# Moving the chunk mask of the attention into spare channels, and moving small work between engines

## The chip, the cores and the metric

The kernel runs on one core of a Trainium2 chip. The metric is device time in microseconds (us); below, TensorE is PE, VectorE is DVE (in the code `V`), ScalarE is ACT (`S_`), GpSimd is POOL (`G`), and SP issues most of the DMAs. The kernel before takes 921.42 us, the median of 3 runs (921.26 to 925.33).

## What is computed

Two layers of a hybrid trunk over 1024 tokens of width 1024, in float32. Each layer normalises its input, projects it with one combined weight, runs three branches (a gated linear recurrence, multi-head latent attention, a spatial gating unit), gates and normalises them, projects them back and adds the residual. The change touches the attention branch:

```python
q = (rms_norm(q_lat, q_norm_g) @ w_uq).reshape(B, S, 6, 96)      # 64 plain + 32 rotary channels
k = concat(k_nope[6 heads x 64], k_pe[32, the same for all heads])
q_pe, k_pe = apply_rope(...)      # (x1 cos - x2 sin, x2 cos + x1 sin), halves of 16
s = q @ k.T * 96 ** -0.5
mask = k_chunk[None, :] <= q_chunk[:, None]      # chunks of 64 tokens
p = softmax(where(mask, s, -inf));  o = p @ v
yb = o * silu(gb)
```

With blocks of 128 queries, the mask leaves out all later blocks of keys; inside the block of the diagonal it hides the second 64 keys from the first 64 queries.

## The kernel before, in words

Every float32 product is made of three matmuls on parts (`mm3`, L123 to L126): a value is split into a rounded high part (ACT writes it) and the remainder (DVE or GpSimd subtracts, `split`, L355 to L358). All matmuls have a stationary operand of 128 by 128.

Per layer, in order: the recurrence's projections, the gating unit's, the latent projection (`toks`, L764 to L800, one step per 128 tokens, which also rotates the shared keys into `ln` and transposes them), then the gate of the attention branch with the loading of `w_uq` (`load_uq`), then the attention, then the output projection (`project`).

The heads use 128 channels per query and key: 64 plain ones, and 64 that carry the rotation as four products of 16 (`cos`, `cos`, `-sin`, `sin`), prepared by a table `MQ` with which each query is multiplied after its projection (`queries`, L893), and by doubled key sums (L776).

The attention runs over 24 units (head h, pair of query blocks j). The loop `for n in range(len(units))` issues, per turn, keys and queries for unit n + 4, `scores` for unit n + 2, and `mixv` for unit n. `scores` makes for each of two blocks i: the score matmuls into one of two PSUM buffers (`pw`), a matmul of the identity with `mask_b` that adds -1e30 on the hidden corner (L929), the negated row maximum on DVE (L936), the exponential on ACT with the row sum (L938), the reciprocal on DVE (L939) and the multiplication by it on GpSimd (L940). `mixv` transposes the probabilities (L960), splits them (L357, L358), multiplies them with the values (L969) into one half of a PSUM buffer `o`, adds the two halves of the partitions (ACT L977, DVE L978) and multiplies the gate in (L981, on DVE for the 13 units of `Y_ON_V`, on GpSimd for the 11 others). `Q_ON_V` lists the queries that DVE splits.

The order of the instructions on each engine isn't that of the program text: a planner with its own costs for each instruction (`schedule_with_timeline_sim=True`) lays them out when the kernel is built, except for those under `keep`. Each engine then runs its list strictly in order.

Of the kernel before, what the change touches and what calls it, by code (L numbers as in the profile page):

```python
# [25 lines left out]
YA, YC, YB = 0, 3, 5  # L26

TWO_PI = 2.0 * np.pi
EXP_C = (1.0, 0.5, 1.0 / 6, 1.0 / 24, 1.0 / 120, 1.0 / 720, 1.0 / 5040)
# [9 lines left out]
W_ON_V = (C_U, C_GC)  # L39
Q_ON_V = ((0, 0), (0, 1), (1, 1), (4, 0))  # L40
Y_ON_V = (2, 4, 5, 6, 8, 9, 13, 14, 16, 19, 20, 21, 23)
# [46 lines left out]
def trunk_kernel(tc, A, out):  # L88
# [54 lines left out]
    G.memset(mhalf, -0.5)  # L143
    mask_b = cst.tile([128, 256], F32R, name="mask_b")
    G.memset(mask_b.bitcast(F32), 0.0)
    G.memset(mask_b[0:64, 192:256].bitcast(F32), -1e30)
    Y = cst.tile([128, 8, T], F32, name="Y")
# [107 lines left out]
    def rope_tables():  # L255
# [44 lines left out]
        V.memset(TQ[:, :, 0:64], SCALE)  # L300
        for o, tab, c in ((64, CK, SCALE), (80, CK, SCALE), (96, SK, -SCALE), (112, SK, SCALE)):
            V.tensor_scalar(out=TQ[:, :, o:o + 16], in0=tab, scalar1=c, scalar2=None, op0=ALU.mult)
        for h in range(2):
# [247 lines left out]
    for l in range(DEPTH):  # L551
# [210 lines left out]
        for t in range(NT):  # L762
            if t % 2 == 0:
                latn.append(FS.take((128, 2, 384)))  # L764
            ln = latn[t // 2][:, t % 2]
            ps = toks(hT, w, t, 352, "P1")
# [8 lines left out]
            V.tensor_tensor(out=r2[:, 1, 16:32], in0=kr[:, 0:16], in1=SK[:, t], op=ALU.mult)  # L775
            V.tensor_tensor(out=ln[:, 192:256].rearrange("p (a b) -> p a b", a=2),  # L776
                            in0=r2[:, 0:1].to_broadcast([128, 2, 32]), in1=r2[:, 1:2].to_broadcast([128, 2, 32]),
                            op=ALU.add)
            r = rsqrt(ms, 2)
# [28 lines left out]
        def load_uq(r0, n, gcol):  # L808
# [4 lines left out]
            g = par[:, gcol:gcol + 1]  # L813
            for o, i, c in ((96, 80, 16), (112, 64, 16), (0, 0, 96)):
                V.tensor_scalar(out=st[:, :, o:o + c], in0=st[:, :, i:i + c], scalar1=g, scalar2=None, op0=ALU.mult)
            i = len(uq)
# [69 lines left out]
        def queries(h, half):  # L886
# [5 lines left out]
            qm = HS.take((128, 512))  # L892
            V.tensor_tensor(out=qm, in0=ps, in1=MQ[:, hs], op=ALU.mult)  # L893
            q = RS.take((128, 2, 512))
# [9 lines left out]
        def scores(h, j):  # L904
# [5 lines left out]
            else:  # L910
                pair = None
            res = []
            for i in (2 * j, 2 * j + 1):
                n = (i + 1) * 128
                o = (i % 4) * 128
                sh, sl = q[:, 0, o:o + 128], q[:, 1, o:o + 128]
                ps = bank("P2") if j >= 2 else pw[:, (i % 2) * 512:(i % 2 + 1) * 512]

                step = n // 2 if n == 640 else 512
                for c0 in range(0, n, step):  # L920
                    w = max(256, min(step, n - c0))
                    diag = c0 <= i * 128 < c0 + step
                    o0 = c0 // step * 512
                    mm3(ps[:, o0:o0 + w], sh, sl, kh[:, c0:c0 + w], kl[:, c0:c0 + w], True, not diag)
                    if diag:

                        d1 = o0 + (i + 1) * 128 - c0
                        d0 = max(o0, d1 - 256)
                        PE.matmul(ps[:, d0:d1], lhsT=identr, rhs=mask_b[:, 256 - (d1 - d0):256], start=False,  # L929
                                  stop=True)  # L930
                if step < 512:
                    sv = ps.rearrange("p (a b) -> p a b", b=512)[:, :, 0:step]
                else:
                    sv = ps[:, 0:n].rearrange("p (a b) -> p a b", a=1)
                mx, sm, rs = SM(1), SM(1), SM(1)
                V.tensor_reduce(out=mx, in_=sv, axis=AX.XY, op=ALU.max, negate=True)  # L936
                p = FS.take((128, 1024)) if j >= 2 else pair[:, i % 2]
                S_.activation(p[:, 0:n].rearrange("p (a b) -> p a b", a=sv.shape[1]), sv, AF.Exp, bias=mx, accum_out=sm)  # L938
# [9 lines left out]
        def mixv(h, j):  # L948
# [27 lines left out]
            tmp = HS.take((128, 256))  # L976
            S_.activation(tmp[mine], o[other], AF.Copy, scale=0.5)  # L977
            V.scalar_tensor_tensor(out=tmp[mine], in0=o[mine], scalar=0.5, in1=tmp[mine],  # L978
                                   op0=ALU.mult, op1=ALU.add)
            yv = Y[mine, YB + h // 2, j * 256:(j + 1) * 256]  # L980
            (V if units.index((h, j)) in Y_ON_V else G).tensor_tensor(out=yv, in0=yv, in1=tmp[mine], op=ALU.mult)  # L981
            HS.give(tmp)
# [174 lines left out]
```

## Time and profile before

| What | us |
|---|---|
| median of 3 runs | 921.42 |
| the profiled execution, its own time | 919.1 |
| its span, first to last instruction | 917.3 |
| PE busy in it | 877.1 |
| DVE busy | 583.9 |
| ACT busy | 520.3 |
| POOL busy | 395.1 |
| granted TensorE clock, mean | 0.994 |

A busy time is the union of an engine's instructions. A matmul's row lasts longer than the slot that it takes: matmuls overlap each other in the array, so that the price of one is read from the distance of two starts, and short waits don't show as idle time. The attention takes about 255 to 380 us in layer 0 and 699 to 825 us in layer 1 (first to last mask matmul).

### The profile page before, as it was taken

The page shows a single profiled execution, that of the slowest core. Times are in us where ns is not written, and L with a number is a line of the kernel's source. Part 1 is how long each engine was busy: PE and PEld are TensorE (multiplying, and loading weights), DVE is VectorE, ACT ScalarE, POOL GpSimd, SP SyncE. Part 2 cuts the span into 40 slices and gives each one's busy share as a digit, 9 for nine tenths or more (in the row PEclk, how much of TensorE's full clock was granted, in tenths as well). Part 3 has the DMA queues.
Part 4 walks back from the last instruction along what each step waited for, and adds up shares of the span by engine and source line. Part 5 has one row for each costly group of instructions (what it writes and reads, how often), then busy time and mean ns, then how long its engine had stood idle before and what let it go on. Part 6 is the DMA issues. An engine that isn't in the chain of part 4 may idle for free. (4 is left out here: it accounts for less than half of the span.)

```text
span 917.3 us, 13660 instructions
## 1 busy us (share of the span) xinstructions
PE 877.1 (96%) x5078; PEld 777.1 (85%) x5078; DVE 583.9 (64%) x1092; ACT 520.3 (57%) x1032; POOL 395.1 (43%) x447
## 2 busy tenths in 40 slices
PE   4999998999999999999999999989989999999996
PEld 3998787998889889888798888889978999988886
DVE  4567955735689898356566498334555989855533
ACT  6446744554767778446444386354466877755312
POOL 4720047564045568356333000675530567655601
PEclk9999999999999999999999999999999999999999
DMA  7201366322000253024323033762200015221321
GB/s 276 56 25 44 108 215 201 132 93 60 14 1 1 93 184 111 9 88 161 106 81 100 1 88 95 275 224 110 59 14 0 1 47 200 77 70 70 138 92 69
DMA packets 45079, 86.93 MB, mean 95 GB/s; under 512 B 8824, under 2 KB 26836, under 8 KB 45012
## 3 DMA queue, kind: packets, MB, share of 16 engines
q1 hardware_dynamic: 35796, 52.50, 18.3%
q0 software_dynamic: 6912, 25.17, 7.8%
q10 hardware_dynamic: 2304, 8.39, 2.3%
q8 instruction: 40, 0.66, 0.3%
q14 instruction: 27, 0.22, 0.1%
HBM read 60.88 MB, written 25.17 MB: 94 GB/s over the span
## 5 line engine op out<-in xcount | busy, mean ns | idle before, releaser
L124 PE MATMUL pw<-R,R 128*128 128x512 f32 (+1 forms) x704 | 258.9, 368 | 6.8 <-DVE R L358 2.4
L126 PE MATMUL pw<-R,R 128*128 128x512 f32 (+1 forms) x704 | 252.7, 359 | 0.1
L125 PE MATMUL pw<-R,R 128*128 128x512 f32 (+1 forms) x704 | 252.7, 359 | 0.0
L124 PE MATMUL pa<-R,R 128*128 128x512 f32 (+3 forms) x540 | 187.2, 349 | 7.9 <-DVE F L708 3.7
L125 PE MATMUL pa<-R,R 128*128 128x512 f32 (+3 forms) x540 | 186.0, 345 | 0.0
L126 PE MATMUL pa<-R,R 128*128 128x512 f32 (+3 forms) x540 | 185.1, 345 | 0.0
L124 PEld LDWEIGHTS pw<-R,R 128*128 128x128 f32 x704 | 134.6, 192 | 26.7 <-ACT F L938 2.7
L126 PEld LDWEIGHTS pw<-R,R 128*128 128x128 f32 x704 | 134.4, 191 | 18.5 <-POOL R L377 0.5
L125 PEld LDWEIGHTS pw<-R,R 128*128 128x128 f32 x704 | 134.8, 192 | 17.2
L124 PEld LDWEIGHTS pa<-R,R 128*128 128x128 f32 x540 | 102.0, 189 | 18.6 <-DVE F L708 3.9
L940 POOL TENSOR_SCALAR F<-F,ring 128x128 f32<-128x128 f32 (+3 forms) x96 | 72.6, 761 | 89.5 <-DVE ring L939 88.1
L126 PEld LDWEIGHTS pa<-R,R 128*128 128x128 f32 x540 | 101.8, 189 | 9.9
L125 PEld LDWEIGHTS pa<-R,R 128*128 128x128 f32 x540 | 102.2, 189 | 8.4
L358 DVE TENSOR_TENSOR R<-pa,R 128x512 fp32r<-128x512 f32 (+1 forms) x120 | 73.9, 629 | 16.5 <-ACT R L357 15.6
L938 ACT ACTIVATE F<-pw,ring 128x128 f32<-128x128 f32 (+3 forms) x96 | 71.1, 743 | 21.0 <-DVE ring L936 18.4
L936 DVE TENSOR_REDUCE ring<-pw 128x1 f32<-128x128 f32 (+3 forms) x96 | 71.6, 749 | 11.4 <-PE pw L929 10.8
L377 POOL TENSOR_TENSOR R<-F,R 128x1024 fp32r<-128x1024 f32 (+1 forms) x24 | 55.2, 2307 | 45.8 <-ACT R L376 45.8
L357 ACT ACTIVATE R<-pa 128x512 fp32r<-128x512 f32 (+1 forms) x120 | 63.7, 554 | 19.6 <-PE pa L960 17.8
L969 PE MATMUL pa<-R,R 128*128 128x256 f32 x480 | 72.1, 288 | 0.5 <-DVE R L358 0.5
L969 PEld LDWEIGHTS pa<-R,R 128*128 128x128 f32 x480 | 63.5, 190 | 3.6 <-DVE R L358 1.1
L960 PE MATMUL pa<-ident,F 128*128 128x128 f32 x432 | 63.6, 273 | 0.7 <-DVE H L893 0.4
L318 ACT ACTIVATE H<-F 128x1024 bf16<-128x1024 f32 (+2 forms) x33 | 31.4, 953 | 55.6 <-DVE F L1004 33.4
(302 smaller groups left out, 1360.5 us busy)
## 6 DMA issues: line engine op xcount, KB each, us to landing
F<-in_w_in SPq DMA_DIRECT2D x24, 512.0 KB, 4.4
F<-in_x SPq DMA_DIRECT2D x13, 512.0 KB, 5.4
F<-in_w_out SPq DMA_DIRECT2D x9, 512.0 KB, 3.5
F<-x SPq DMA_DIRECT2D x8, 512.0 KB
Y<-in_w_out SPq DMA_DIRECT2D x7, 512.0 KB, 3.6
x<-F SPq DMA_DIRECT2D x7, 512.0 KB, 4.1
out_y<-F SPq DMA_DIRECT2D x7, 512.0 KB, 2.7
Y<-in_w_in SPq DMA_DIRECT2D x6, 512.0 KB, 3.6
```

The source lines that it names most:

```text
L124: PE.matmul(ps, lhsT=sh, rhs=mh, start=start, stop=False)
L125: PE.matmul(ps, lhsT=sh, rhs=ml, start=False, stop=False)
L126: PE.matmul(ps, lhsT=sl, rhs=mh, start=False, stop=stop)
L318: order(S_.activation(q.bitcast(BF16)[:, c], xs[i % len(xs)].rearrange("p a b -> p (a b)")[:, c], AF.Square, scale=1.0 / 32, accum_out=ms[ ...
L357: S_.activation(h, src, AF.Copy)
L358: (eng or G).tensor_tensor(out=lo, in0=src, in1=h.bitcast(F32), op=ALU.subtract)
L377: self.eng.tensor_tensor(out=lo, in0=st, in1=h.bitcast(F32), op=ALU.subtract)
L936: V.tensor_reduce(out=mx, in_=sv, axis=AX.XY, op=ALU.max, negate=True)
L938: S_.activation(p[:, 0:n].rearrange("p (a b) -> p a b", a=sv.shape[1]), sv, AF.Exp, bias=mx, accum_out=sm)
L940: G.tensor_scalar(out=p[:, 0:n], in0=p[:, 0:n], scalar1=rs, scalar2=1.0, op0=ALU.mult, op1=ALU.mult)
L960: PE.transpose(pv[:, c, i * 128:(i + 1) * 128], p[i][:, b * 128:(b + 1) * 128], ident)
L969: PE.matmul(o, lhsT=sv, rhs=pt[:, part, c * 256:(c + 1) * 256], start=(b == 0 and part == 0), stop=(b == nb - 1 and part == 1))
```

## The change

The hidden corner is written as a product: the query gets one extra channel per block of 128 tokens (channels 112 to 119), which is 1 for the first 64 queries of its block and 0 elsewhere; the key gets -2^100 in the same channel for the second 64 keys of its block. To free 16 channels, the rotation is written with three products of 16 in place of four. The mask matmul and `mask_b` go. The ones reach the queries through the table `MQ` and a constant column `qoff` that is added in the multiplication by `MQ`.

Beside this: the two blocks of a unit share one reciprocal (2 columns) after both exponentials; for the 13 units of `Y_ON_V` the sum of the two halves of `o` is made by a second ACT copy and a GpSimd addition, where DVE did it in one instruction; and of the four queries per layer that DVE split, two go to GpSimd.

```diff
-Q_ON_V = ((0, 0), (0, 1), (1, 1), (4, 0))
+Q_ON_V = ((0, 0), (0, 1))
...
-    G.memset(mask_b.bitcast(F32), 0.0)
-    G.memset(mask_b[0:64, 192:256].bitcast(F32), -1e30)
+    mkey = cst.tile([128, NT, 16], F32, name="mkey")
+    G.memset(mkey, 0.0)
+    G.memset(mkey.rearrange("p t f -> p (t f)")[64:128, 0::17], HIDE)
+    qoff = cst.tile([128, 1], F32, name="qoff")
+    V.tensor_reduce(out=qoff, in_=ident[:, QMASK:QMASK + 8], axis=AX.X, op=ALU.add)
...
-        for o, tab, c in ((64, CK, SCALE), (80, CK, SCALE), (96, SK, -SCALE), (112, SK, SCALE)):
-            V.tensor_scalar(out=TQ[:, :, o:o + 16], in0=tab, scalar1=c, scalar2=None, op0=ALU.mult)
+        V.tensor_scalar(out=TQ[:, :, 96:112], in0=SK, scalar1=SCALE, scalar2=None, op0=ALU.mult)
+        for o, op in ((64, ALU.subtract), (80, ALU.add)):
+            V.scalar_tensor_tensor(out=TQ[:, :, o:o + 16], in0=CK, scalar=SCALE, in1=TQ[:, :, 96:112], op0=ALU.mult,
+                                   op1=op)
+        V.memset(TQ[:, :, QMASK:128], 0.0)
+        V.memset(TQ.rearrange("p t f -> p (t f)")[0:64, QMASK::129], 1.0)
...
+                G.tensor_copy(latn[-1][:, :, 240:256], mkey[:, t:t + 2])
...
-            V.tensor_tensor(out=ln[:, 192:256].rearrange("p (a b) -> p a b", a=2),
-                            in0=r2[:, 0:1].to_broadcast([128, 2, 32]), in1=r2[:, 1:2].to_broadcast([128, 2, 32]),
-                            op=ALU.add)
+            V.tensor_tensor(out=ln[:, 192:224], in0=r2[:, 0], in1=r2[:, 1], op=ALU.add)
+            V.tensor_tensor(out=ln[:, 224:240], in0=ln[:, 192:208], in1=ln[:, 208:224], op=ALU.add)
...
-            for o, i, c in ((96, 80, 16), (112, 64, 16), (0, 0, 96)):
-                V.tensor_scalar(out=st[:, :, o:o + c], in0=st[:, :, i:i + c], scalar1=g, scalar2=None, op0=ALU.mult)
+            V.tensor_scalar(out=st[:, :, 0:96], in0=st[:, :, 0:96], scalar1=g, scalar2=None, op0=ALU.mult)
+            V.tensor_tensor(out=st[:, :, 96:112], in0=st[:, :, 64:80], in1=st[:, :, 80:96], op=ALU.subtract)
+            V.memset(st[:, :, QMASK:128], 0.0)
...
-            V.tensor_tensor(out=qm, in0=ps, in1=MQ[:, hs], op=ALU.mult)
+            V.scalar_tensor_tensor(out=qm, in0=ps, scalar=qoff, in1=MQ[:, hs], op0=ALU.add, op1=ALU.mult)
...
-                    mm3(ps[:, o0:o0 + w], sh, sl, kh[:, c0:c0 + w], kl[:, c0:c0 + w], True, not diag)
-                    if diag:
-                        d1 = o0 + (i + 1) * 128 - c0
-                        d0 = max(o0, d1 - 256)
-                        PE.matmul(ps[:, d0:d1], lhsT=identr, rhs=mask_b[:, 256 - (d1 - d0):256], start=False,
-                                  stop=True)
+                    mm3(ps[:, o0:o0 + w], sh, sl, kh[:, c0:c0 + w], kl[:, c0:c0 + w], True, True)
...
-                V.reciprocal(out=rs, in_=sm)
-                G.tensor_scalar(out=p[:, 0:n], in0=p[:, 0:n], scalar1=rs, scalar2=1.0, op0=ALU.mult, op1=ALU.mult)
                 res.append(p)
+            V.reciprocal(out=rs, in_=sm)
+            for i, p in enumerate(res):
+                n = (2 * j + i + 1) * 128
+                G.tensor_scalar(out=p[:, 0:n], in0=p[:, 0:n], scalar1=rs[:, i:i + 1], scalar2=1.0, op0=ALU.mult,
+                                op1=ALU.mult)
...
+            on_v = units.index((h, j)) in Y_ON_V
+            S_.activation(tmp[mine, 0], o[other], AF.Copy, scale=0.5)
+            if on_v:
+                S_.activation(tmp[mine, 1], o[mine], AF.Copy, scale=0.5)
+                G.tensor_tensor(out=tmp[mine, 0], in0=tmp[mine, 1], in1=tmp[mine, 0], op=ALU.add)
+            else:
+                V.scalar_tensor_tensor(out=tmp[mine, 0], in0=o[mine], scalar=0.5, in1=tmp[mine, 0],
+                                       op0=ALU.mult, op1=ALU.add)
+            (V if on_v else G).tensor_tensor(out=yv, in0=yv, in1=tmp[mine, 0], op=ALU.mult)
```

## Rows read from the trace of the kernel before

**Rows 1.** The page's first part: busy time, share of the span and instructions of each engine.

```profile
PE 877.1 (96%) x5078; PEld 777.1 (85%) x5078; DVE 583.9 (64%) x1092; ACT 520.3 (57%) x1032; POOL 395.1 (43%) x447
```

**Rows 2.** Windows: busy time (and instructions) of each engine in the dense stretch of each layer's attention, and their sum; behind it one stretch in the tail of layer 1's attention, from a table by 10 us.

```profile
255.40:367.00 111.60, 109.84 (x738) 100.42 (x737) 97.92 (x211) 85.84 (x203) 69.42 (x103) 1.00 0.24 80
712.00:815.60 103.60, 103.08 (x706) 95.21 (x704) 91.83 (x195) 81.33 (x188) 67.58 (x99) 1.00 0.26 87
sum 215.20, PE 212.92 PEld 195.62 DVE 189.75 ACT 167.17 POOL 137.00; mean PE 106.46 PEld 97.81 DVE 94.88 ACT 83.59 POOL 68.50
...
840.00:850.00 10.00, 10.00 (x54) 8.56 (x53) 8.33 (x8) 5.47 (x11) 7.46 (x6) 1.00 0.29 100
```

**Rows 3.** Waits of PE (us in total, times, longest): in 255 to 366 us, then in 710 to 816 us.

```profile
PE pw L124 <- ACT F L938: 0.7, 2, 0.4
PE pa L960 <- DVE H L893: 0.4, 1, 0.4
...
PE pw L124 <- ACT F L938: 0.3, 1, 0.3
```

**Rows 4.** Groups of instructions by line with shapes kept apart (count, busy us and mean ns of one, idle time before): the mask matmul and its weight load.

```profile
L929 PE MATMUL pw<-mask_b,ident 128*128 128x256 f32 x84 | 23.7, 282 | 0.0
L929 PEld LDWEIGHTS pw<-mask_b,ident 128*128 128x128 f32 x96 | 18.1, 188 | 1.0
```

**Rows 5.** Timeline (start us, length us): a mask matmul of 256 columns between its neighbours, and one of 128 columns.

```profile
301.56 0.28 PE L126 MATMUL pw<-R,R 128*128 128x256 f32 x1
301.68 0.28 PE L929 MATMUL pw<-mask_b,ident 128*128 128x256 f32 x1
301.80 0.49 PE L960 MATMUL pa<-ident,F 128*128 128x128 f32 x3
...
308.78 0.22 PE L929 MATMUL pw<-mask_b,ident 128*128 128x128 f32 x1
308.84 0.45 PE L124 MATMUL pa<-R,R 128*128 128x512 f32 x1
```

**Rows 6.** Groups of instructions by line with shapes kept apart: the work that the change moves, and its nearest relatives.

```profile
L978 DVE SCALAR_TENSOR_TENSOR H<-pa,H 64x256 f32<-64x256 f32 x48 | 20.1, 418 | 12.7 <-ACT H L977 12.0
L977 ACT ACTIVATE H<-pa 64x256 f32<-64x256 f32 x48 | 18.2, 379 | 14.6 <-PE pa L969 13.8
L981 POOL TENSOR_TENSOR Y<-Y,H 64x256 f32<-64x256 f32 x22 | 16.7, 758 | 17.3 <-DVE H L978 16.9
L981 DVE TENSOR_TENSOR Y<-Y,H 64x256 f32<-64x256 f32 x26 | 12.5, 480 | 0.7
L939 DVE RECIPROCAL ring<-ring 128x1 f32<-128x1 f32 x96 | 14.6, 156 | 11.2 <-ACT F L938 10.5
L358 DVE TENSOR_TENSOR R<-H,R 128x512 fp32r<-128x512 f32 x8 | 6.0, 745 | 2.2 <-PE pa L126 2.2
L358 POOL TENSOR_TENSOR R<-H,R 128x512 fp32r<-128x512 f32 x16 | 20.7, 1296 | 2.3 <-ACT R L357 2.1
L893 DVE TENSOR_TENSOR H<-pa,MQ 128x512 f32<-128x512 f32 x24 | 16.4, 684 | 3.9 <-PE pa L891 3.3
L414 DVE SCALAR_TENSOR_TENSOR Y<-H,pa 128x512 f32<-128x512 f32 x16 | 10.8, 682 | 13.7 <-ACT H L412 13.7
```

**Rows 7.** ACT's longest wait in 255 to 366 us (us in total, times, longest), and the two longest steps of one block of scores, from the groups.

```profile
ACT F L938 <- DVE ring L936: 11.2, 13, 2.0
...
L936 DVE TENSOR_REDUCE ring<-pw 128x1 f32<-128x1024 f32 x12 | 14.6, 1218 | 3.6 <-PE pw L929 3.6
...
L938 ACT ACTIVATE F<-pw,ring 128x1024 f32<-128x1024 f32 x12 | 13.4, 1116 | 5.5 <-DVE ring L936 5.5
```

**Rows 8.** Lines one by one (duration in ns: shortest, median, longest; first and last start): a DVE instruction with two inputs in SBUF (L776), one with one input in PSUM (L978), the gate product (L981); then, from the timeline, the longest L776 and the GpSimd instruction that ran beside it.

```profile
L776 DVE TENSOR_TENSOR F<-rt x16: 208/416/2175, 169.4 to 674.9; 128x64 f32<-128x64 f32 x16
...
L978 DVE SCALAR_TENSOR_TENSOR H<-pa,H x48: 393/422/428, 271.2 to 848.4; 64x256 f32<-64x256 f32 x48
...
L981 DVE TENSOR_TENSOR Y<-Y,H x26: 404/422/1225, 278.8 to 848.8; 64x256 f32<-64x256 f32 x26
...
169.37 2.17 DVE L776 TENSOR_TENSOR F<-rt 128x64 f32<-128x64 f32 x1
...
169.07 2.39 POOL L377 TENSOR_TENSOR R<-F,R 128x1024 fp32r<-128x1024 f32 x1 [0.56 <-ACT R L376]
```

**Rows 9.** The stages ahead of the attention: small DVE instructions of the latent projection and of `load_uq` line by line (ns: shortest, median, longest), then PE's longest waits in 600 to 690 us and in 140 to 255 us.

```profile
L773 DVE SCALAR_TENSOR_TENSOR rt<-pa,SK x16: 162/164/166, 169.1 to 672.3; 128x16 f32<-128x16 f32 x16
...
L815 DVE TENSOR_SCALAR F<-F,par x12: 257/272/1262, 229.5 to 675.0; 128x96 f32<-128x96 f32 x8, 128x576 f32<-128x576 f32 x4
...
PE pw L124 <- DVE R L358: 2.4, 1, 2.4
PE pa L124 <- DVE Y L414: 1.5, 1, 1.5
...
PE pa L124 <- DVE F L708: 3.7, 1, 3.7
```

**Rows 10.** Timeline at the start: the two memsets of `mask_b` on GpSimd, and PE's first matmul.

```profile
0.91 0.31 POOL L145 MEMSET mask_b<- 128x256 f32 x1
...
1.51 0.14 POOL L146 MEMSET mask_b<- 64x64 f32 x1
...
4.64 0.45 PE L189 MATMUL pa<-ident,H 128*128 128x128 f32 x1 [4.64 <-DMA H<-in_pre_norm_g]
```

More of the change, by code (lines that the diff above doesn't have):

```diff
@@ L26 @@
 YA, YC, YB = 0, 3, 5
+QMASK, HIDE = 112, -2.0 ** 100
 TWO_PI = 2.0 * np.pi
@@ L143, in trunk_kernel @@
     G.memset(mhalf, -0.5)
-    mask_b = cst.tile([128, 256], F32R, name="mask_b")
-    G.memset(mask_b.bitcast(F32), 0.0)
-    G.memset(mask_b[0:64, 192:256].bitcast(F32), -1e30)
+    mkey = cst.tile([128, NT, 16], F32, name="mkey")
[3 more added lines that the diff above has]
+    V.tensor_reduce(out=qoff, in_=ident[:, QMASK:QMASK + 8], axis=AX.X, op=ALU.add)
     Y = cst.tile([128, 8, T], F32, name="Y")
@@ L912, in scores @@
             res = []
+            sm, rs = SM(2), SM(2)
             for i in (2 * j, 2 * j + 1):
@@ L921, in scores @@
                     w = max(256, min(step, n - c0))
-                    diag = c0 <= i * 128 < c0 + step
                     o0 = c0 // step * 512
-                    mm3(ps[:, o0:o0 + w], sh, sl, kh[:, c0:c0 + w], kl[:, c0:c0 + w], True, not diag)
-                    if diag:
-                        d1 = o0 + (i + 1) * 128 - c0
-                        d0 = max(o0, d1 - 256)
-                        PE.matmul(ps[:, d0:d1], lhsT=identr, rhs=mask_b[:, 256 - (d1 - d0):256], start=False,
-                                  stop=True)
+                    mm3(ps[:, o0:o0 + w], sh, sl, kh[:, c0:c0 + w], kl[:, c0:c0 + w], True, True)
                 if step < 512:
@@ L934, in scores @@
                     sv = ps[:, 0:n].rearrange("p (a b) -> p a b", a=1)
-                mx, sm, rs = SM(1), SM(1), SM(1)
+                mx = SM(1)
                 V.tensor_reduce(out=mx, in_=sv, axis=AX.XY, op=ALU.max, negate=True)
                 p = FS.take((128, 1024)) if j >= 2 else pair[:, i % 2]
-                S_.activation(p[:, 0:n].rearrange("p (a b) -> p a b", a=sv.shape[1]), sv, AF.Exp, bias=mx, accum_out=sm)
-                V.reciprocal(out=rs, in_=sm)
-                G.tensor_scalar(out=p[:, 0:n], in0=p[:, 0:n], scalar1=rs, scalar2=1.0, op0=ALU.mult, op1=ALU.mult)
+                S_.activation(p[:, 0:n].rearrange("p (a b) -> p a b", a=sv.shape[1]), sv, AF.Exp, bias=mx,
+                              accum_out=sm[:, i % 2:i % 2 + 1])
                 res.append(p)
+            V.reciprocal(out=rs, in_=sm)
[3 more added lines that the diff above has]
+                                op1=ALU.mult)
             probs[h, j] = res, [pair] if j < 2 else res
@@ L975, in mixv @@
             mine, other = slice(r0, r0 + 64), slice(64 - r0, 128 - r0)
[L976 to L979, printed above, removed]
+            tmp = HS.take((128, 2, 256))
             yv = Y[mine, YB + h // 2, j * 256:(j + 1) * 256]
-            (V if units.index((h, j)) in Y_ON_V else G).tensor_tensor(out=yv, in0=yv, in1=tmp[mine], op=ALU.mult)
+            on_v = units.index((h, j)) in Y_ON_V
[7 more added lines that the diff above has]
+            (V if on_v else G).tensor_tensor(out=yv, in0=yv, in1=tmp[mine, 0], op=ALU.mult)
             HS.give(tmp)
```

## The prediction

> **What bounds the kernel now.** I began with the page's engine shares: PE is busy 877.1 us of 917.3, 96% [rows 1]. No other engine is over 64%. But a matmul's row overlaps its neighbours, and an average hides stages, so I next took windows over the dense stretch of each attention, where the change acts. There PE is busy 212.92 of 215.20 us, DVE 189.75 (88%), ACT 167.17 (78%), POOL 137.00 (64%) [rows 2]. The reader is to see two things in this row: PE sets the pace, since its idle time is only 215.20 - 212.92 = 2.28 us, and DVE is close behind it. PE's waits say the same: the longest sum in layer 0's stretch is 0.7 us, for the exponential that frees a score buffer, in layer 1's 0.3 us [rows 3]. So a slot that PE no longer needs there should come off the span, provided the other engines keep up with a PE that is some 5% faster.
>
> **The change part by part.** The sum is made against the profiled execution, 919.1 us, of which 917.3 are the span. The median of the runs shown is 921.42, that is 2.3 more; I add this at the end.
>
> *Mask matmuls.* 96 go, 84 of 256 columns and 12 of 128 [rows 4]. Their mean of 282 ns isn't their price, since the row overlaps the next. The price is the distance of starts: 301.68 to 301.80, 0.12 us, for 256 columns, 308.78 to 308.84, 0.06 us, for 128 [rows 5]. So 84 x 0.12 + 12 x 0.06 = 10.8 us. The weight loads (18.1 us in all) lie beside the matmul before them and add nothing. No matmul grows: the score matmuls already use all 128 rows [rows 5], so that the spare channels cost PE nothing. Bounds: 0 (all turned into waiting) and, from the whole idle time of the dense stretches falling too, 10.8 + 2.3 = 13.1.
>
> *Reciprocals by pairs.* 48 of 96 go, 48 x 0.156 = 7.5 us of DVE, and some of the 10.5 us that DVE waited for ACT in front of them [rows 6]. The first block's probabilities are ready later, by up to the second block's reduction and exponential, 1.2 + 1.1 us [rows 7]. They are read two units later; a unit takes about 111.6 / 24 = 4.7 us of the stretch [rows 2]. That cover hides it; without it, up to 48 x 2.3 us would be at stake. I take 0 on the path.
>
> *Sums of `o`.* For 26 units DVE loses 26 x 0.418 = 10.9 us, ACT gains a copy, 26 x 0.379 = 9.9 us, POOL an addition of the shape of L981 on POOL, 26 x 0.758 = 19.7 us [rows 6]. The new wait: DVE's gate product (L981) now stands behind a GpSimd addition, which stands behind whatever GpSimd has begun. Queued behind the product on DVE are the splits of the transposed probabilities and the maxima of the scores, for which PE waits in turn. Bounds: 0 when the planner puts enough other DVE work ahead of it, 0.76 us per unit and more when not. In the last unit of a layer the chain gets 0.38 + 0.76 - 0.42 = 0.7 us longer; behind it PE projects without a gap (10.00 of 10 us [rows 2]), so this costs nothing.
>
> *Query splits.* Four go from DVE, 4 x 0.745 = 3.0 us, to POOL, 4 x 1.296 = 5.2 us [rows 6]. The queries are made four units ahead, so 0 on the path; 0.6 us each if that cover fails.
>
> *Multiplication by `MQ`.* A product with PSUM becomes add-and-multiply: 684 ns for the plain product, 682 for a scalar_tensor_tensor of the same shape from PSUM [rows 6]. So 0, with 24 x 2 ns as the distance of the two rows either way.
>
> *Balance in the dense stretches.* DVE 189.75 - 7.5 - 10.9 - 3.0 = 168.4 us, ACT 177.1, POOL 137.0 + 19.7 + 5.2 = 161.9. Over 215.2 - 10.8 = 204.4 us that is 82%, 87% and 79%. (Seven mask matmuls and a few units lie in the tails; I count them here as if inside.) DVE gets looser though PE gets faster, ACT becomes the second engine. So I see no engine that takes PE's place, and leave PE's waits as they are.
>
> *Ahead of the attention.* Per step of the latent projection, one DVE addition becomes two smaller ones, and four small GpSimd copies per layer write the key's mask. A small DVE instruction takes 0.16 us [rows 9]: 16 x 0.16 = 2.6 us more of DVE at most, against up to 16 x (0.42 - 0.21) = 3.4 us less, median against shortest, if the shorter ones escape the stretching of L776 [rows 8]. A copy on GpSimd lies between 0.14 us and 0.31 us, the memsets at the start [rows 10]; it can hold up the small GpSimd instructions behind it by as much. In `load_uq` two products of 96 columns become one difference and a memset: the same 0.27 us each [rows 9]. At the start the memsets are as many as before and end 3 us ahead of PE's first matmul at 4.64 us, which waits for a DMA [rows 10]. All 0, with bounds of 1 us either way.
>
> *The planner.* All lists of instructions are laid out anew. Outside the attention PE's longest waits are 3.7, 2.4 and 1.5 us [rows 9], each one place where an instruction stands behind another on DVE. Such places can go or come: 0, with bounds of 3 us either way, estimated from these rows.
>
> Sum: 919.1 - 10.8 = 908.3, plus 2.3 for the median: **910.6 us**, 1.2% faster.
>
> **A rule that speaks against it.** L776 reads two inputs from SBUF, and lasts from 208 to 2175 ns; the longest began at 169.37 while GpSimd ran a 2.39 us instruction from 169.07 on. L978, with one input in PSUM, stays within 393 to 428 ns [rows 8]. The Trainium skill ("SBUF — State Buffer", section "Who interferes with whom") says that a DVE instruction with two SBUF inputs and a GpSimd instruction that reads SBUF exclude each other for a whole instruction. The trace agrees with that. The gate product (L981) on DVE is such an instruction, and it now runs when GpSimd has just finished its addition and turns to the next thing. By the rows it has mostly escaped: median 422 ns, longest 1225 [rows 8].
>
> **The rivals.**
>
> 1. *DVE waits behind GpSimd (slower).* The gate product blocks DVE until GpSimd's addition is done, at 26 places. If the length of the addition reaches PE each time, 26 x 0.76 = 19.8 us is lost against 10.8 won: 921.4 + 9.0 = 930.4. It decides from 10.8 / 26 = 0.42 us per place that reaches PE. For it: POOL goes from 64% to 79%, and the order on DVE is fixed by a planner's costs. Against it: DVE will have some 36 us without work in the stretches (204.4 - 168.4), and a unit gives the planner 4.7 us to place the product. 9%.
>
> 2. *DVE stays as full as it was.* Each of the 26 gate products is stretched as the longest of them was, by 1225 - 422 = 0.8 us [rows 8]: 20.9 us, as much as the relief of 21.4. DVE then has 189.3 us in 204.4, 93%, the score buffers turn over too slowly (ACT waits 11.2 us for the maximum already [rows 7]), and half of the mask's time comes back as PE's waits: 921.4 - 5.4 = 916.0. The half is a choice between none and all. For it: the rows on L776. Against it: a mean of 480 ns against a median of 422 leaves room for one or two stretched ones in 26 [rows 6, 8]. 20%.
>
> 3. *The relief also empties PE's waits.* PE's idle 2.28 us of the stretches goes, with shorter waits of ACT for DVE: 910.6 - 2.3 = 908.3, and a little less with the planner's luck. 13%.
>
> 4. *The change doesn't do what it says:* were the mask's product to need matmuls of its own, PE's count would stay; the diff leaves none, so this gets no share.
>
> **How the numbers follow.** Forecast 58%, rivals 1 to 3 with 9, 20 and 13%. About 0.5% (4.6 us) is what a measurement can tell from no change, so faster means under 916.8, slower over 926.0. The forecast and rival 3 are faster, as is half of rival 2, which straddles the bound: 58 + 13 + 10 = 81%. Slower is rival 1 but for its mildest part: 8%. The rest, 11%, is the same. The range takes the forecast with the planner's 3 us downward and rival 3 (905.5), and upward to rival 2 and a little over it (917.5); rival 1 and the upper end of rival 2 stay outside.
>
> **What would show it.** PE has 96 matmuls less, 4982. The two attentions (first to last score) are each about 5.4 us shorter, and the stages before and after keep their lengths within 1.5 us each. L939 appears 48 times, L978 22 times. PE's waits in the dense stretches stay near 2 us; DVE is near 82% there, ACT near 87%. It is wrong if DVE shows waits for POOL of over 0.4 us per gate product and PE shows waits for DVE's splits behind them (rival 1), if the gate product's mean goes from 480 towards 1200 ns (rival 2), or if a wait of some us appears in a stage ahead of the attention that the change hardly touches (the planner).

## The result and the profile after

The kernel after takes 932.35 us, the median of 5 runs (928.6 to 933.18), against 921.42 before: 1.0109 times as long, 95% interval 1.0085 to 1.0134. The forecast of 910.6 us is missed on the other side of no change, and the range with it. The profiled execution took 928.6 us, the fastest of the five; its span is 926.8.

The page's engine shares, which answer to [rows 1], and the same two dense stretches as in [rows 2]:

```profile
PE 875.1 (94%) x4982; PEld 769.2 (83%) x4982; DVE 573.3 (62%) x1032; ACT 530.4 (57%) x1058; POOL 418.4 (45%) x485
```

```profile
255.40:367.00 111.60, 105.65 (x681) 93.99 (x680) 93.11 (x172) 87.90 (x209) 79.05 (x115) 0.98 0.24 81
712.00:815.60 103.60, 95.87 (x612) 84.62 (x612) 85.92 (x154) 79.27 (x185) 73.19 (x106) 0.99 0.24 82
sum 215.20, PE 201.52 PEld 178.62 DVE 179.03 ACT 167.17 POOL 152.24; mean PE 100.76 PEld 89.31 DVE 89.52 ACT 83.58 POOL 76.12
```

The 96 matmuls are gone, as promised (4982 are left), but what is left isn't done sooner: the two stretches hold 681 + 612 matmuls where they held 738 + 706, 62 less than the 89 of the mask explain, and PE's idle time there rose from 2.28 to 13.68 us. No other engine took its place as the fullest: DVE fell to 83%, ACT stayed at 78%, POOL rose from 64 to 71%. PE's waits (us in total, times, longest), which answer to [rows 3], in 255 to 366 us and then in 690 to 830 us:

```profile
PE pa L979 <- DVE R L369: 2.6, 2, 1.9
PE pw L126 <- ACT F L944: 1.4, 3, 0.8
...
PE pa L979 <- DVE R L369: 2.2, 2, 2.0
PE pa L970 <- DVE R L369: 1.9, 2, 1.3
PE pw L126 <- ACT F L944: 1.8, 4, 0.7
```

L979 is the multiplication with the values (before L969), L970 the transposition of the probabilities (before L960), L126 the first of a product's three matmuls (before L124), and L369 the subtraction in `split` (before L358). The timeline (start us, length us) shows the longest of these waits, in layer 0; layer 1 repeats it at 805 to 810 us:

```profile
349.48 2.11 POOL L950 TENSOR_SCALAR F<-F,ring 128x896 f32<-128x896 f32 x2
...
350.47 3.24 DVE L996 TENSOR_TENSOR Y<-Y,H 64x256 f32<-64x256 f32 x1
...
352.14 1.28 POOL L369 TENSOR_TENSOR R<-H,R 128x512 fp32r<-128x512 f32 x1
...
353.64 0.41 DVE L942 TENSOR_REDUCE ring<-pw 128x1 f32<-128x256 f32 x1
353.97 0.54 DVE L369 TENSOR_TENSOR R<-pa,R 128x384 fp32r<-128x384 f32 x1
354.08 0.47 ACT L944 ACTIVATE F<-pw,ring 128x256 f32<-128x256 f32 x1 [2.90 <-DVE ring L942]
...
354.56 0.61 PE L979 MATMUL pa<-R,R 128*128 128x256 f32 x3 [1.93 <-DVE R L369]
```

Read it from the second row: a gate product (L996), 0.42 us of work, stays on DVE for 3.24 us while POOL runs two normalizations and a query split. The row maximum and the split queued behind it start at 353.64 and 353.97; ACT has waited 2.90 us, PE 1.93 us. Behind the wait in either layer the clock falls; the second window lies ahead of layer 1's attention (windows; the column before the DMA share is the granted clock):

```profile
354.00:360.00 6.00, 5.44 (x30) 5.26 (x31) 3.87 (x9) 4.30 (x10) 4.12 (x9) 0.72 0.10 33
676.00:682.00 6.00, 5.47 (x18) 4.44 (x19) 2.42 (x6) 1.22 (x3) 0.18 (x1) 0.72 0.00 0
812.00:818.00 6.00, 5.90 (x33) 5.65 (x34) 3.33 (x6) 2.81 (x7) 2.88 (x5) 0.72 0.00 0
```

A mean of 0.72 over 6 us means that a part of the window ran at the lower of the two levels, and costs 0.28 x 6 = 1.7 us each time. In the kernel before, all three windows show 1.00.

To see where PE's time went I added up, over each attention (first to last transposition), the distances of successive matmul starts: as *slots* up to the undisturbed distance for their width (0.125 us for 256 columns, in proportion for 320 and 384, 0.23 for 512, 0.11 at 128), as *waiting* what exceeds it, a low clock included. One profiled execution each, both layers together, with the experiments told below:

| kernel | slots | waiting | sum |
|---|---|---|---|
| before | 245.7 | 14.1 | 259.8 |
| after | 235.2 | 33.1 | 268.3 |
| a1, mask on spare channels alone | 232.8 | 21.7 | 254.5 |
| c1, mask matmuls left out | 237.4 | 24.3 | 261.7 |
| d1, same work, other lists | 244.8 | 13.6 | 258.4 |
| d2, d1's lists, mask left out | 235.9 | 23.0 | 258.9 |
| d4, a1 without held products | 236.1 | 22.0 | 258.2 |
| e1, DVE relieved | 243.5 | 12.6 | 256.1 |
| e2, DVE and PE relieved | 237.4 | 21.0 | 258.4 |

So the 10.5 us of slots did come off, and 19.0 us of waiting came in: +8.5 of the span's +9.5 us. The table has two limits. A single execution can lie several us from its kernel's median (d1's, 926.16, and d4's, 928.01, are the slowest of their ten). And other work can move into or out of the attentions: over the whole span, counted in the same way, the slots fall by some 10 us both from before to after and from d1 to d2.

### The profile page after: what moved, and what is told of

Same layout as the page of the kernel before. It is cut to its first block, busy times and chain, and to the rows that moved or that the text cites. A ratio compares the mean times of both kernels' runs of the same rounds, so it can differ in the third digit from the quotient of the medians.

```text
span 926.8 us, 13510 instructions
## 1 busy us (share of the span) xinstructions
PE 875.1 (94%) x4982; PEld 769.2 (83%) x4982; DVE 573.3 (62%) x1032; ACT 530.4 (57%) x1058; POOL 418.4 (45%) x485
## 4 chain that ended last, share of the span: by engine, by line
PE 62%; DVE 12%; ACT 7%; DMA 7%; POOL 6%; issue 4%; SPq 0%; POOLq 0%; DVEq 0%; ACTq 0%
PE pw L126 10%; PE pw L128 10%; PE pw L127 10%; PE pa L126 7%; PE pa L127 7%; PE pa L128 7%; PE pa L979 4%; PE pa L970 4%; DMA F<-in_w_in 2%; ACT R L368 2%; ACT F L944 1%; DVE ring L942 1%; DVE Y L996 1%; POOL ring L135 1%; DVE R L369 1%
## 5 line engine op out<-in xcount | busy, mean ns | idle before, releaser
L126 PE MATMUL pw<-R,R 128*128 128x512 f32 (+1 forms) x704 | 260.0, 370 | 9.3 <-ACT F L944 3.3
L126 PE MATMUL pa<-R,R 128*128 128x512 f32 (+3 forms) x540 | 187.4, 350 | 8.6 <-DVE F L719 3.8
L126 PEld LDWEIGHTS pw<-R,R 128*128 128x128 f32 x704 | 135.1, 192 | 30.8 <-ACT F L944 6.2
L126 PEld LDWEIGHTS pa<-R,R 128*128 128x128 f32 x540 | 102.3, 190 | 20.1 <-DVE F L719 4.0
L369 DVE TENSOR_TENSOR R<-pa,R 128x512 fp32r<-128x512 f32 (+1 forms) x120 | 73.4, 632 | 37.2 <-ACT R L368 36.5
L979 PE MATMUL pa<-R,R 128*128 128x256 f32 x480 | 76.4, 291 | 6.8 <-DVE R L369 4.8
L979 PEld LDWEIGHTS pa<-R,R 128*128 128x128 f32 x480 | 65.4, 190 | 12.4 <-DVE R L369 6.4
L970 PE MATMUL pa<-ident,F 128*128 128x128 f32 x432 | 66.7, 280 | 2.5 <-DVE R L369 2.3
```

The costliest lines, as they stand in the source:

```text
L126: PE.matmul(ps, lhsT=sh, rhs=mh, start=start, stop=False)
L369: (eng or G).tensor_tensor(out=lo, in0=src, in1=h.bitcast(F32), op=ALU.subtract)
L970: PE.transpose(pv[:, c, i * 128:(i + 1) * 128], p[i][:, b * 128:(b + 1) * 128], ident)
L979: PE.matmul(o, lhsT=sv, rhs=pt[:, part, c * 256:(c + 1) * 256], start=(b == 0 and part == 0), stop=(b == nb - 1 and part == 1))
```

## The experiments

Ratios are to the kernel before on the same chip, with 95% intervals. Over the study the median of the kernel before lay between 920.8 and 922.6, single runs from 917.9 to 927.6. The letters of the theories hold within each batch.

### Parts alone and parts undone

**a1, the mask on spare channels alone**: the change with the three edits of a2, a3 and a4 together, so that sums, reciprocals and query splits are as before. Two places of its difference from the kernel before:

```diff
             qm = HS.take((128, 512))
-            V.tensor_tensor(out=qm, in0=ps, in1=MQ[:, hs], op=ALU.mult)
+            V.scalar_tensor_tensor(out=qm, in0=ps, scalar=qoff, in1=MQ[:, hs], op0=ALU.add, op1=ALU.mult)
...
-                        PE.matmul(ps[:, d0:d1], lhsT=identr, rhs=mask_b[:, 256 - (d1 - d0):256], start=False,
-                                  stop=True)
...
```

> The kernel before with the chunk mask on the spare channels and nothing else: reciprocals, output sums and query splits as before. Theory H (the gate products on DVE are held by GpSimd since the sums are made there, and PE waits behind them): the mask alone brings what its slots cost, 911 us (908 to 915), and no gate product on DVE inside the dense stretches lasts over 1 us. Theory P (any new list of the planner may cost such waits): anywhere from 912 to 930. Theory M (the mask itself costs elsewhere, by the longer multiplication by MQ or the new key channels): 925 or more.

Measured: 920.37 us, 0.9983 (0.9965 to 1.0002). The mask's gain is missing although GpSimd gets nothing in the attentions, and one product is still held there, for 2.53 us at 799.7 us. In the profiled execution the attentions are 5.3 us shorter than before (table), but the stretch between them (last transposition of layer 0 to first of layer 1) is 6.4 us longer, 326.7 against 320.3: 2.7 us are slots of work that has moved there, 3.7 us waiting.

**a2, the change with the sums back on DVE.**

```diff
-            if on_v:
-                S_.activation(tmp[mine, 1], o[mine], AF.Copy, scale=0.5)
-                G.tensor_tensor(out=tmp[mine, 0], in0=tmp[mine, 1], in1=tmp[mine, 0], op=ALU.add)
...
+            V.scalar_tensor_tensor(out=tmp[mine], in0=o[mine], scalar=0.5, in1=tmp[mine],
+                                   op0=ALU.mult, op1=ALU.add)
...
```

> The changed kernel with the output sums back on DVE (one instruction from PSUM), the pairs of reciprocals and the two query splits on GpSimd kept. Theory H: the long gate products and the 2 us waits of PE behind them go, 912 us (908 to 917). If the sums are innocent: 928 to 933 as the changed kernel.

Measured: 925.66 us, 1.0035 (1.0013 to 1.0057). This lies between the two expectations: 6.7 us come back, and a product of 2.65 us remains (at 803.8 us).

**a3, the change with a reciprocal per block again** (the 48 paired ones become 96).

```diff
+                V.reciprocal(out=rs, in_=sm)
+                G.tensor_scalar(out=p[:, 0:n], in0=p[:, 0:n], scalar1=rs, scalar2=1.0, op0=ALU.mult, op1=ALU.mult)
                 res.append(p)
-            V.reciprocal(out=rs, in_=sm)
...
```

> The changed kernel with one reciprocal per block again. Theory H with the sums as cause: the gate products still stand behind GpSimd, but two normalisations no longer come back to back, so the longest hold shrinks from 3.3 to about 2 us: 922 to 931. A theory that the pairs are the cause (both normalisations late and in one piece): 912 to 917.

Measured: 931.09 us, 1.0087 (1.0055 to 1.0118): the pairs are not the cause. The longest product didn't shrink to about 2 us either, it takes 3.72 us.

**a4, the change with the two query splits back on DVE.**

```diff
-Q_ON_V = ((0, 0), (0, 1))
+Q_ON_V = ((0, 0), (0, 1), (1, 1), (4, 0))
```

> The changed kernel with the two query splits back on DVE. Theory H: GpSimd has 2.6 us less per layer, little else changes, 927 to 932. A theory that GpSimd is simply too full (72% in the dense stretches): 918 to 924.

Measured: 921.05 us, 0.9999 (0.9979 to 1.0019). Four splits in the whole kernel, 5.2 us of POOL, make a difference of 11 us, with the lists laid out anew. The time is in the range of the theory that GpSimd was too full. In this kernel the longest gate product on DVE is 1.45 us, after it was 3.31:

```profile
L996 DVE TENSOR_TENSOR Y<-Y,H x26: 406/422/1450, 275.3 to 853.5; 64x256 f32<-64x256 f32 x26
```

**b3 and b4, the sums alone and the splits alone, in the kernel before**: the edits of a2 and of a4 the other way round.

> The kernel before (mask matmuls, single reciprocals, four query splits on DVE) with the 13 output sums per layer on ACT and GpSimd. Theory H: products move behind GpSimd's additions and some are held, 921 to 928. If DVE's relief is worth anything by itself: 915 to 919.

> The kernel before with two more query splits per layer on GpSimd and nothing else. Theory H: GpSimd runs 5 us more of back-to-back work in the stretches and more products may be held, 921 to 927. Theory P (the list of the kernel before is a lucky one, and any new list loses a few us): 923 to 930 here as in the sums alone, without a cause in the parts.

Measured: 925.59 us, 1.0051 (1.0027 to 1.0074), and 925.12 us, 1.0034 (1.0016 to 1.0052). Both lose by themselves. They don't add up simply: with the mask and the pairs, the sums cost nothing (c4, below, 923.15; a4 921.05) and the splits 2.5 us (a2), both together 9.2 us (932.35 - 923.15).

**c4, mask and pairs**: the change with the edits of a2 and a4 together, neither sums nor splits.

> The mask on spare channels and the reciprocals by pairs, with the output sums and the two query splits as before. Theory H (what GpSimd is given costs, what VectorE is spared is free): 917 to 920.5 us, no gate product on VectorE over 2.6 us. Rival J (the pairs cost by themselves: the first probabilities of a pair wait for the second's exponentials): 921.5 us or more, GpSimd's normalizations starting later behind their exponentials than in the mask-only kernel.

Measured: 923.15 us, 1.0014 (0.9985 to 1.0044). The time is in the range of rival J, but the interval reaches down to no change. What DVE is spared by the pairs gains nothing. One product is held for 2.88 us (at 800.1 us), with neither sums nor splits moved.

### The gate product

**b1, DVE's gate product reads `o` in PSUM** and one column of GpSimd's sum (it multiplies with another value).

```diff
...
+                V.scalar_tensor_tensor(out=yv, in0=o[mine], scalar=tmp[mine, 0, 0:1], in1=yv, op0=ALU.add,
+                                       op1=ALU.mult)
...
```

> The changed kernel, in which the 13 gate products per layer on DVE read one operand from PSUM and one column of the GpSimd sum, so that they have one SBUF tensor input but still wait for GpSimd's addition; the gate's product is computed from another operand than in the reference. Theory H (a DVE instruction with two SBUF inputs is held while GpSimd runs one instruction after the other): no product lasts over 0.6 us, the 2 us waits of PE behind them go, 915 to 922 us. Rival W (the wait for GpSimd's addition is what costs, my rival 1): 928 to 933, and the idle time of DVE in front of the product stays. Rival P (only the planner's list decides): no telling, 918 to 932, with long products or without.

Measured: 943.95 us, 1.0252 (1.0214 to 1.029). This run can't decide on the held product, since `o` now stays occupied until GpSimd has added, and the next unit's values need it. It is 943.95 - 932.35 = 11.6 us slower than the change. That the occupied `o` is the reason is likely but not shown: PE's waits put down to these products are 2.4 us in both layers.

**b2, all gate products on GpSimd.**

```diff
-            (V if on_v else G).tensor_tensor(out=yv, in0=yv, in1=tmp[mine, 0], op=ALU.mult)
+            G.tensor_tensor(out=yv, in0=yv, in1=tmp[mine, 0], op=ALU.mult)
```

> The changed kernel with all gate products on GpSimd, so that DVE has none with two SBUF inputs in the attention except the query splits. Theory H: no hold of over 1.3 us left in the dense stretches, 914 to 922 us although GpSimd has 13 x 0.75 us more per layer and DVE 13 x 0.42 us less. Rival W and a theory that GpSimd is too full: 932 or more.

Measured: 930.92 us, 1.0095 (1.0065 to 1.0125). No product can be held, but POOL gets 26 products of 0.758 us more [rows 6], so that this too leaves the question open.

**d4, the mask alone, with DVE's sums written back over `o`**, so that each of its gate products has one operand in PSUM (difference from a1, in part).

```diff
+            s = (o if on_v else tmp)[mine]
+            V.scalar_tensor_tensor(out=s, in0=o[mine], scalar=0.5, in1=tmp[mine], op0=ALU.mult, op1=ALU.add)
...
```

> The mask-only kernel with VectorE's 13 output sums of a layer written back over o, so that the gate product behind each has one operand outside SBUF. Theory H (held gate products are what eats the mask's gain): no product over 0.7 us in the attentions, and 912 to 917 us. Rivals P and F: the holds go and the time stays at 919 to 923 us.

Measured: 923.47 us, 1.0019 (0.9997 to 1.0041). The holds are gone:

```profile
L987 DVE TENSOR_TENSOR Y<-Y,pa x26: 390/424/426, 282.3 to 860.3; 64x256 f32<-64x256 f32 x26
```

and the time isn't better than a1's. So the mask's gain can be missing without a held product. That holds cost nothing where they stand doesn't follow: here `o` stays occupied until the product has read it, as in b1, and d2 below shows what one hold took.

### The mask's 10.8 us

**c1, the kernel before with the mask matmuls left out and nothing in their place.**

```diff
-                    if diag:
...
-                        PE.matmul(ps[:, d0:d1], lhsT=identr, rhs=mask_b[:, 256 - (d1 - d0):256], start=False,
-                                  stop=True)
...
```

> The kernel before with its 96 mask matmuls left out and nothing put in their place (no key is hidden within a block pair, so the result differs there). Theory S (slots: TensorE sets the pace of the attentions, and what the mask-only kernel lost came from the spare channels' extra work around it): 910 to 912 us, and TensorE's waits in the two attentions stay within 2 us of before's 14. Rival F (following engines: the attentions are paced by the softmax on VectorE, ScalarE and GpSimd, the mask matmuls filled gaps): 917 to 922 us, with TensorE's matmul slots 10 us shorter and its waits in the attentions 6 to 10 us longer. In between, each by its share.

Measured: 922.88 us, 1.0035 (1.0015 to 1.0056). 96 matmuls less, and not faster at all. So the gain goes missing without the spare channels too. One product is held for 4.00 us (at 347.1 us), and PE waits 3.15 us behind it.

**c2, every mask matmul twice.**

```diff
                         PE.matmul(ps[:, d0:d1], lhsT=identr, rhs=mask_b[:, 256 - (d1 - d0):256], start=False,
+                                  stop=False)
+                        PE.matmul(ps[:, d0:d1], lhsT=identr, rhs=mask_b[:, 256 - (d1 - d0):256], start=False,
                                   stop=True)
```

> The kernel before with every mask matmul issued twice (the second adds -1e30 to the same corner again). Theory S: the second set costs what the first does on TensorE, about 10.8 us: 930 to 933 us. Rival F: the second set fills waiting time that is left (14 us in the attentions), 922 to 926 us.

Measured: 936.3 us, 1.018 (1.0154 to 1.0206), more than either expected. In the attentions the profiled execution is 6.5 us longer (slots 254.4, waiting 11.9). Another 11.9 us lie in the stretch between them, which the edit doesn't touch (332.1 us against 320.3); 5.1 of these are time lost at the lower clock (13.6 us at half the clock in that stretch, 3.4 before), for the rest I have no cause. In the attentions, then, PE's added work is mostly paid, 6.5 us for 8.7 us of slots.

**c3, a1 with the loading of the query weights on ACT and GpSimd.**

```diff
-            V.tensor_scalar(out=st[:, :, 0:96], in0=st[:, :, 0:96], scalar1=g, scalar2=None, op0=ALU.mult)
+            S_.activation(st[:, :, 0:96], st[:, :, 0:96], AF.Copy, scale=g)
...
```

> The mask-only kernel with the scaling of the query weights on ScalarE and the difference and the zeros of the spare channels on GpSimd. Theory L (in the stage ahead of layer 1's attention VectorE's longer list there, 576 columns scaled in one instruction beside GpSimd, costs a wait and then a half clock of 3.4 us on TensorE): 916 to 919 us, and no half-clock stretch between 670 and 690 us. Rival (the wait there only moves to another operation): 919.5 to 921.5 us with the half-clock stretch still there.

Measured: 926.13 us, 1.0079 (1.0047 to 1.0111). It costs instead of gaining, and the low clock stays (0.79 in 676 to 684 us). The theory falls.

**d1 and d3, the same matmuls as before, the mask's put second and third of its chunk's four.** The lists come out a little otherwise on every engine. d1:

```diff
                     PE.matmul(ps[:, o0:o0 + w], lhsT=sh, rhs=kh[:, kq], start=True, stop=False)
+                    if diag:
+                        PE.matmul(ps[:, d0:d1], lhsT=identr, rhs=mask_b[:, 256 - (d1 - d0):256], start=False,
+                                  stop=False)
                     PE.matmul(ps[:, o0:o0 + w], lhsT=sh, rhs=kl[:, kq], start=False, stop=False)
...
```

> The kernel before with each mask matmul issued second of its chunk's four matmuls instead of last: the same instructions, but the planner's lists come out otherwise on every engine. Theory P (before's lists are a good draw, and another list of the same work costs some us by itself): 923 to 928 us, TensorE's waits in the attentions 4 to 10 us longer than before's 14. Rival F (the work that follows the scores sets the attentions' time, whatever the list): 920 to 922 us, waits within 2 us of before's.

> The kernel before with each mask matmul issued third of four: the same work once more with a third set of lists. Theory P: anywhere from 920 to 930 us, as the list falls, and not what d1 takes. Rival F: 920 to 922 us.

Measured: 921.97 us, 0.9988 (0.9968 to 1.0008), and 920.38 us, 0.9989 (0.9973 to 1.0006). The theory that the lists of the kernel before were a good draw gets no support. It isn't tested hard: with the mask matmuls left aside, d1's list for DVE differs from before's at 59 of 1092 places and PE's at 146 of 4982, d3's at 55 and 166, but c1's at 256 and 601. So lists that differ as much as those of c1 or of the change may still cost something by themselves.

**d2, d1 with the mask matmuls taken out after the lists were made.** Every other instruction keeps its place.

```diff
+    gone = {m.ins.name for m in MASKS}
+    for blk in nc.main_func.blocks:
+        rest = [i for i in blk.instructions if i.name not in gone]
+        if len(rest) < len(blk.instructions):
+            blk.instructions = rest
```

> The kernel of d1 with its 96 mask matmuls taken out after the lists were made, so that every other instruction stays in its place on its engine (no key is hidden within a block pair). Theory P: with the list held, TensorE's time comes off, 8 to 11 us below d1. Rival F: the gaps stay and grow, 0 to 3 us below d1.

Measured: 922.17 us, 0.9999 (0.9979 to 1.002), 0.2 us from d1. This is the cleanest pair of the study: 8.9 us of slots less, 9.4 us of waiting more. PE's waits in 255 to 366 us, for d1 and then for d2:

```profile
PE pw L925 <- ACT F L940: 0.7, 2, 0.4
PE pa L962 <- DVE H L893: 0.4, 1, 0.4
PE pa L962 <- DVE R L358: 0.3, 1, 0.3
```

```profile
PE pw L925 <- ACT F L940: 3.8, 3, 3.2
PE pa L962 <- DVE R L358: 0.8, 2, 0.5
PE pa L962 <- DVE H L893: 0.8, 1, 0.8
```

The same instructions are waited for, each longer: the exponential that frees a score buffer, the splits and the queries from DVE. The longest of these waits has a cause of its own, a held gate product with no GpSimd work added. The timeline shows the same product in d1 and then in d2:

```profile
356.63 0.45 DVE L983 TENSOR_TENSOR Y<-Y,H 64x256 f32<-64x256 f32 x1
357.13 2.11 POOL L942 TENSOR_SCALAR F<-F,ring 128x896 f32<-128x896 f32 x2
```

```profile
352.89 4.01 DVE L983 TENSOR_TENSOR Y<-Y,H 64x256 f32<-64x256 f32 x1
353.29 2.11 POOL L942 TENSOR_SCALAR F<-F,ring 128x896 f32<-128x896 f32 x2
355.37 1.25 POOL L358 TENSOR_TENSOR R<-H,R 128x512 fp32r<-128x512 f32 x1
358.13 0.70 PE L925 MATMUL pw<-R,R 128*128 128x512 f32 x1 [3.17 <-ACT F L940]
```

In d1 the product is done 0.05 us before POOL's normalizations begin. In d2 they begin 0.40 us after its start, and it stays until 356.90. Since all lists agree, the two executions can also be compared instruction by instruction. By d1's times, d2's lead (how much earlier it starts the same instruction) grows in layer 0 from 1.8 us (at 255, before the first mask matmul) to 3.7 (at 352, after 39 of the 48 mask matmuls, 4.4 us by the prediction's prices). At 362 it is -0.5: the hold and the lower clock behind it (0.72 over 358 to 364 us in d2) took 4.2 us back. In layer 1, without such a hold, the lead grows from -0.6 (at 700) to 2.1 (at 849), 2.7 us for 5.4 us of mask matmuls. So in this pair about half of the slots came off where no product was held for long, and one hold took most of what came off in the two layers. It is one execution of each; the medians differ by 0.2 us.

The other runs point the same way. With the mask matmuls in place the longest product lasts 1.0 to 1.7 us (before, b3, c2, d1, d3) or 2.34 (b4). Without them, and with products that read SBUF alone, it lasts 2.5 to 4.0 us in eight kernels of nine (a1, a2, a3, c1, c3, c4, d2, after) and 1.45 us in a4.

**e1 and e2, DVE relieved: its 13 sums and gate products per layer left out**, in the kernel before and together with the mask matmuls.

```diff
-            V.scalar_tensor_tensor(out=tmp[mine], in0=o[mine], scalar=0.5, in1=tmp[mine],
-                                   op0=ALU.mult, op1=ALU.add)
...
+            if units.index((h, j)) not in Y_ON_V:
+                V.scalar_tensor_tensor(out=tmp[mine], in0=o[mine], scalar=0.5, in1=tmp[mine],
+                                       op0=ALU.mult, op1=ALU.add)
...
+                G.tensor_tensor(out=yv, in0=yv, in1=tmp[mine], op=ALU.mult)
```

> The kernel before with VectorE's 13 output sums and gate products of each layer left out (these parts of the gated output stay ungated), so VectorE is spared 23 us in the attentions and nothing goes to another engine; the mask matmuls stay. Theory V (the attentions have two bounds of nearly one size, TensorE and VectorE with the releases between them): 917 to 920 us, since TensorE's slots stay. Rival B (the score buffers, filled again only after row maximum and exponentials, set the pace): 912 to 917 us if it is VectorE's queue that delays the row maxima, otherwise no change.

> The same with the 96 mask matmuls left out as well, so both engines are relieved and GpSimd and ScalarE get nothing. Theory V: now TensorE's 10.8 us come off, 907 to 912 us, with TensorE's waits in the attentions back near 14 us. Rival B (a third thing holds the pace): 916 to 921 us, waits in the attentions 22 us or more.

Measured: 921.26 us, 0.9996 (0.9976 to 1.0016), and 918.24 us, 0.9956 (0.9932 to 0.9981). Neither engine alone moves the time; both together give 4.3 us of the 10.8. Theory V wanted 917 to 920 and 907 to 912 us, with PE's waits back near 14 us. What came is close to rival B, a third thing that holds the pace: no change in e1, and in e2 a time within 916 to 921 us with 21.0 us of waiting. In the attentions e2's profiled execution is even 2.3 us longer than e1's (258.4 against 256.1). What keeps the rest is spread over short waits (e2, 690 to 830 us):

```profile
PE pw L124 <- ACT F L932: 1.9, 5, 0.6
PE pa L963 <- DVE R L358: 0.2, 1, 0.2
```

## Why the prediction was wrong

**The mask's term, -10.8 us.** The price was right: some 10 us of slots came off. The step that failed is "a slot that PE no longer needs there should come off the span, provided the other engines keep up", and with it "leave PE's waits as they are": PE's waiting in the attentions went from 14.1 to 33.1 us, and with the mask matmuls alone left out (c1) to 24.3. I tested the proviso by shares of busy time, 82, 87 and 79%, and these can't show it. A share says that an engine has time in a stretch, not that its result is there when PE turns to it. In the kernel before, PE's 2.28 idle us looked like a pace that PE sets. d2 against d1 tests just this, with every list the same: 0.2 us by the medians. The traces of that pair show two losses. About half of the slots turned into short waits for the chain behind PE (row maximum, exponential, score buffer; transposition, split), and most of the other half went in one held product with low clock behind it. Leaving out the work of DVE's side gave nothing (e1), leaving out both 4.3 us (e2). That PE and DVE are two bounds of one size would fit this in part, but e1 and e2 came out nearer to a third thing. Which part of the chain keeps the rest isn't settled.

**The sums, 0 on the path, and the query splits, 0.** Alone they cost about 4 us each (b3, b4). "So I see no engine that takes PE's place" was true and beside the point. The two longest waits of PE come through a gate product that DVE could not finish beside GpSimd: 1.93 and 2.00 us, with 1.7 us of low clock behind each, 7.3 us by these rows. A third product, of 2.87 us at 762.7, stands before the wait of 1.3 us. That the splits or the sums lead to such holds is not shown. a4 has no product over 1.45 us and takes 11 us less, but kernels without moved sums or splits have holds too (a1 2.53, c4 2.88, c1 4.00 us), and the query splits beside the three products here are not ones that the change moved. So the place of part of the loss is shown, and why sums and splits together cost 9 us stays open.

**Reciprocals by pairs, 0.** Held within what can be measured: a3 is 1.3 us from the change, and c4 2.8 us above a1 with overlapping intervals. **Multiplication by `MQ`, 0:** it takes longer than the row that I took for it (682 ns, with a constant scalar in place of a column), 24 x 0.06 = 1.4 us on DVE:

```profile
L905 DVE SCALAR_TENSOR_TENSOR H<-pa,qoff,MQ x24: 728/743/752, 246.1 to 802.0; 128x512 f32<-128x512 f32 x24
```

**Balance.** ACT was to be at 87% and is at 78, DVE at 82 and is at 83, POOL at 79 and is at 71: the forecast divided by a stretch 10.8 us shorter, and the stretch got longer. **Ahead of the attention, 0:** in 668 to 684 us some of the clock is lost (0.79 in 676 to 684), but c1, which changes nothing there, shows the same.

**The planner, 0 ± 3.** Not contradicted by the times of d1 and d3, whose lists differ little from before's. In the profiled executions the stretch between the attentions takes 320.3 us before, 319.9 in b4, 321.7 in d3, and 323 to 332 in all others, so 3 us were too few for it. **The signs:** the counts came as promised; the two attentions, each to be 5.4 us shorter, went from 132.8 to 131.1 us and from 127.0 to 137.2 by the sums above. The other stages were to keep their lengths within 1.5 us; the stretch between the attentions became 4.2 us longer, the one behind them 3.4 us shorter.

**The rivals.** Rival 1 came nearest in time (930.4), by luck, since its road is not what the trace shows: DVE waits for GpSimd's addition 13.9 us in all, but in the dense stretches only 1.0 of them; the others are in the tails, where PE has the projection to do. Rival 2 has the mechanism that the trace shows, a gate product stretched beside GpSimd. Its mean is 858 ns (22.3 us / 26), between the 480 of before and the 1200 that it named:

```profile
L996 DVE TENSOR_TENSOR Y<-Y,H x26: 403/422/3305, 279.0 to 864.8; 64x256 f32<-64x256 f32 x26
```

It reckoned with 26 products at 1.2 us and DVE at 93%. What came was a median of 422 and three products of 2.9 to 3.3 us in bad places: not the load on DVE, but what is queued behind one instruction. And its "half of the mask's time comes back" was too mild: by the medians all of it does, in d4 without any held product.

## What to carry to other kernels

An engine that is busy 99% of a stretch need not be what sets its length. Before counting on a gain there, leave the work out, with nothing in its place, and measure; leave out work of the engine behind it as well. Taking the instructions out after the planner has made its lists separates the work from the lists, and lets two traces be compared instruction by instruction. Before work goes to GpSimd to relieve VectorE, look at what stands behind VectorE's two-SBUF-input instructions in its list.

## What the hardware showed that I had not expected

A held VectorE instruction can outlast the GpSimd instruction beside it. In the kernel after, the product at 350.47 ends at 353.71, 2.1 us after the normalizations (to 351.59), and past the split that GpSimd began only at 352.14; before, the longest gate product was 1.23 us [rows 8]. The Trainium skill ("SBUF — State Buffer", section "Who interferes with whom") lets the two exclude each other for a whole instruction. The trace agrees with that in kind (with one operand in PSUM, d4, no product lasts over 426 ns), but here the hold lasted several GpSimd instructions.

A wait of about 2 us on PE was followed by a stretch at the lower clock at both places in the kernel after (0.72 over 6 us, 1.7 us lost), so that a wait's price was nearly twice its length. This isn't so each time: after the wait of 2.52 us in a1 (at 802.9 us) the granted clock stayed at 1.00.
